# Two-layer hybrid encoder on one core: mixer A's projections and seven gate blocks in seven-product form, in a phase at the head of each layer

## The chip, the cores and the metric

One core of one Trainium2 chip runs the whole program. The metric is device microseconds of one execution, median of several runs.

## The reference

Two layers, 512 tokens, width 1024, all in float32. Each layer does this:

```
xn = rmsnorm(x, norm1_g[l]);  h = xn @ w_in[l]        # split into the inputs of four mixers
y_a = gdn_mixer(...)    # A: gated DeltaNet, q/k/v (512 columns each) through a 5-tap convolution and silu
y_b = diff_mixer(...)   # B: differential attention
y_c = swa_mixer(...)    # C: windowed attention
y_d = mlstm_mixer(...)  # D: mLSTM
branch = einsum('bsnw,nwd->bsnd', ys, w_branch[l])
gate   = sigmoid(einsum('bsd,dne->bsne', xn, w_gate[l]))
x = x + sum_n(gate * branch) @ w_out[l]
xn = rmsnorm(x, norm2_g[l]);  x = x + square(relu(xn @ w_mlp1[l])) @ w_mlp2[l]
```

A last rmsnorm follows. Every dense product `x @ w` of these is the subject here.

## The kernel before

**Dense products.** For precision each float32 operand is split into a high part and a low part; a product takes three matmuls (high x high, high x low, low x high). A weight block of 512 KB comes by DMA on SP's queue into a tile `wr` (two buffers), ScalarE copies it to the rounded high part `wh` (L292), VectorE subtracts to the low part `wl` (L293, "a split" below, in two pieces of 128x512 per block); `wh` and `wl` have three buffers each. `Item.get` (L244) gives a block and puts the splits of the next one (two ahead in the MLP) in the queues before it. The plain forms are `run_b` (L400; 128 columns, 24 matmuls of 512 tokens; q, k, v of mixer A), `run_b2` (L415; 256 columns, 48 matmuls of 512 tokens; gates `g`, branches `m`) and `run_a` (L374; 256 columns, 96 matmuls of 256 columns).

**The seven-product form.** The first MLP product (`M1`, L790) treats a group of 512 columns as 2x2 blocks of weights and 2x2 blocks of tokens and input halves, and makes it from seven products of half-size blocks in place of eight. Four weight blocks arrive in two large tiles `wq`; GpSimd makes the four combinations S1 to S4 (L809, two subtractions or additions of 128x512 each); the combinations T1 to T4 of the tokens are made once (`Norm.sums`, L492). Each product is 24 matmuls of 256 columns (L832 to L834); results are put together by six additions on VectorE (L850), one on GpSimd (L851) and two copies on ScalarE (L839).

**Order.** A list `ORDER` (L40) says in which order the dense items of a layer come. The letters: `ga0` is gate a, columns 0 to 255; `Ak0` mixer A's k projection, head 0; `sm` the small projections; `z`, `dv`, `do`, `dqk`, `B`, `C`, `Ck` the other mixers' projections; `gd` gate d; `ma`, `md` branch products with the gate (`m`); `xb`, `xc` gate and branch product in turn. Each item is a generator that gives 1300 or 1310 after each 1.3 us of matmuls. `until(label)` runs items up to a label. `drive(mixer)` runs a mixer: between its steps the mixer gives a gap in ns, and `fill` runs dense steps until the gap is paid. An item may wait for a mark (`dqk` for `s`, the end of mixer A's scans; `ma` for `ya`, the end of mixer A; likewise `md`, `mb`, `mc`); if the next item waits, `fill` gives nothing, and items behind it aren't looked at. The gaps, from `G` (L33) and the loops: mixer A 0.5, eight of 0.3, 2.5, four times 20 of 1.6, nine of 1.5, then 4 x 1.3 + 1.5 + 4 x 1.6 us; mixer D 57.1 in all; a half of mixer B 21.6, and some 9 to drain its transposes before the second; mixer C 73.9 (32 units, each a front and a step three units later of 0.95, and eight closings). The compiler then orders each engine's instructions from this program order, by what its own model says is ready; it may take a later instruction first where its data and buffers are there.

**The places of the change.** Before mixer A starts, `until("Aq3")` runs ga0, the q and k projections, `sm`, ga1 and ga2. `conv` (L942) copies a projection from PSUM, and runs the convolution: one scaled copy on ScalarE, four multiply-adds (L958) and, behind a tanh, a last step (L962) on VectorE. `merge` (L595) makes gates and branches; gate d's tanh goes to DRAM (L613) and comes back before `md`. Gates of b and c are used where they are made.

Of the kernel before, what the change touches and what calls it, by code (L numbers as in the profile page):

```python
# [10 lines left out]
F32 = mybir.dt.float32  # L11
# [6 lines left out]
P = 128  # L18
# [12 lines left out]
NAR = 26  # L31
NBG = 13
# [7 lines left out]
ORDER = ("ga0 Ak0 Aq0 sm ga1 Ak1 Ak2 Aq1 Aq2 Ak3 ga2 Aq3 Av z0 ga3 dv0 "  # L40
         "z1 dv1 do0 do1 gd dqk ma B0 Ck md B1 C0 C1 xb xc")
# [72 lines left out]
def encoder(ctx: ExitStack, tc: tile.TileContext, a: dict, out: bass.AP, dbg: dict = None):  # L114
# [8 lines left out]
    ar = ctx.enter_context(tc.tile_pool(name="ar", bufs=NAR))  # L123
    bg = ctx.enter_context(tc.tile_pool(name="bg", bufs=NBG))
# [112 lines left out]
    class Item:  # L237
# [285 lines left out]
    def build(l, L):  # L523
        w_in = a["w_in"][l]
        n1 = L.n1 = Norm(a["norm1_g"][l])
        L.n2 = Norm(a["norm2_g"][l], True)
        xf = lambda: n1.x

# [31 lines left out]
        def projA(kind, hs):  # L560
            for h in hs:
                def ev(ps, kind=kind, h=h):
                    conv(L, kind, h, ps)
                Item(f"A{kind}{h}{l}", wl_b(w_in, {"q": O_AQ, "k": O_AK, "v": O_AV}[kind] + h * P), run_b(xf, ev))
# [30 lines left out]
        def merge(n, key, part="gm", ccs=range(4)):  # L595
            yf = lambda: ([L.y[key][0][:, k, :] for k in range(4)], [L.y[key][1][:, k, :] for k in range(4)])
            for cc in ccs:
                st = {}

                def gev(b, bank, cc=cc, st=st):  # L600
                    kt = cc * 2 + b
                    if key == "a":
                        if kt == 0:
                            mgb = [B4(s="mg") for _ in range(2)]
                            L.mg = [mgb[k // 4][:, k % 4, :] for k in range(KD)]
                        act.activation(L.mg[kt], bank, AF.Tanh, scale=0.5)
                        return
                    sg = A(s="gs")
                    act.activation(sg, bank, AF.Tanh, scale=0.5)
                    if part == "g":  # L610
                        if key not in L.gsp:
                            L.gsp[key] = dr.tile([8, P, S], F32, tag=f"gs{key}{l}", name=f"gs{key}{l}")
                        act.dma_start(L.gsp[key][kt], sg)  # L613
# [3 lines left out]
                def bev(b, bank, cc=cc, st=st):  # L617
# [17 lines left out]
                f0 = key == "a" and cc == 0  # L635
                gi = lambda: Item(f"g{key}{cc}{l}", wl_a(a["w_gate"][l, :, n], cc * 256, KD),
                                  run_b2(xf, KD, gev, hook1 if f0 else None))
# [15 lines left out]
        bi = "abcd".index  # L653
        for o in ORDER.split():
            if o == "sm":
                small()
            elif o[0] == "A":
                projA(o[1], range(4) if len(o) == 2 else [int(o[2])])
# [131 lines left out]
        def M1(fg):  # L790
            st = {}
            qv = lambda t, i: t[:, i * 1024:(i + 1) * 1024].rearrange("p (k c) -> p k c", k=4)

            def slot(n):
                t, i = {"22": ("a", 0), "11": ("a", 1), "21": ("b", 0), "12": ("b", 1), "S3": ("b", 0),
                        "S1": ("a", 1), "S2": ("b", 0), "S4": ("b", 0)}[n]
                if t not in st:
                    st[t] = B(s="wq")
                return qv(st[t], i)

            def dma(n):
                i, j = int(n[0]) - 1, int(n[1]) - 1
                c0 = fg * 512 + i * 256
                nc.sync.dma_start(slot(n), w1[j * 512:(j + 1) * 512, c0:c0 + 256].rearrange("(k p) c -> p k c", p=P))

            def comb(dst, x, y, op):
                d, x, y = slot(dst), slot(x), slot(y)
                for k in range(0, 4, 2):
                    pool.tensor_tensor(d[:, k:k + 2], x[:, k:k + 2], y[:, k:k + 2], op=op)  # L809
            E = dict(kt=4, nc=256)  # L810
            pS3 = lambda: comb("S3", "11", "21", ALU.subtract)
            pS2 = lambda: comb("S2", "22", "S3", ALU.subtract)
            pS1 = lambda: comb("S1", "S2", "11", ALU.add)
            pS4 = lambda: comb("S4", "12", "S2", ALU.subtract)
# [936 lines left out]
```

## Time and profile before

| | |
|---|---|
| runs | 2354.01 us median of 3 (2350.83 to 2354.09) |
| the profiled execution's own time | 2351.57 us |
| its span (first to last instruction) | 2349.8 us |
| TensorE busy | 2285.3 us (97%) |
| VectorE, ScalarE, GpSimd busy | 1582.2, 1187.5, 747.6 us |
| granted TensorE clock | 0.996 of full speed |

In the rows below PE is TensorE, DVE VectorE, ACT ScalarE, POOL GpSimd, and L293 is line 293. Names stand as out<-in. A matmul's row gives 0.28 or 0.39 us, but matmuls are pipelined: the next one starts 0.12 or 0.23 us later.

### The profile page before, as it was taken

What the parts mean: (1) busy time and instruction counts of PE and PEld (TensorE: products, weight loads), DVE (VectorE), ACT (ScalarE), POOL (GpSimd) and SP (SyncE); (2) the same over time, 40 slices, a digit from 0 to 9 for tenths busy, and PEclk for the clock granted to TensorE, in tenths of its full rate; (3) what the DMA queues carried; (4) which work ended last, traced back from release to release, by engine and by line L of the source; (5) the groups of instructions that cost most, each with busy time, mean ns of one, the idle gap of its engine ahead of it and who ended that gap; (6) DMA issues with size and microseconds to landing.
All of it is one profiled execution on the core that took longest, in us unless ns stands there. A gap on an engine that the chain in (4) does not pass through costs nothing. (4 is left out here: it accounts for less than half of the span.)

```text
span 2349.8 us, 43335 instructions
## 1 busy us (share of the span) xinstructions
PE 2285.3 (97%) x16992; PEld 2083.2 (89%) x16992; DVE 1582.2 (67%) x2988; ACT 1187.5 (51%) x2777; POOL 747.6 (32%) x806
## 2 busy tenths in 40 slices
PE   7999999999999999999999999999999999999998
PEld 6879987989888989999987799879898889899998
DVE  5774547685786477677767745587767854867775
ACT  4565444654665264344445654365546643534443
POOL 1135552132232134343200555412313310434341
PEclk9999999999999999999999999999999999999999
DMA  6322131222122523333323112321221234233322
GB/s 149 99 46 64 55 95 57 60 88 80 51 71 74 160 71 122 95 109 108 111 74 90 55 55 64 91 63 52 93 82 55 72 106 131 90 97 109 99 82 90
DMA packets 234779, 200.72 MB, mean 85 GB/s; under 512 B 31696, under 2 KB 223824, under 8 KB 234576
## 3 DMA queue, kind: packets, MB, share of 16 engines
q1 hardware_dynamic: 231408, 192.75, 27.5%
q10 hardware_dynamic: 2304, 4.20, 0.5%
q8 instruction: 133, 2.18, 0.4%
q0 software_dynamic: 864, 1.02, 0.2%
q14 instruction: 70, 0.57, 0.1%
HBM read 190.04 MB, written 8.39 MB: 84 GB/s over the span
## 5 line engine op out<-in xcount | busy, mean ns | idle before, releaser
L293 DVE TENSOR_TENSOR wl<-wr,wh 128x512 fp32r<-128x512 f32 x540 | 400.4, 762 | 183.4 <-ACT wh L292 176.1
L292 ACT CAST wh<-wr 128x512 fp32r<-128x512 f32 x540 | 317.0, 621 | 219.0 <-PE pd L436 59.2
L392 PE MATMUL pd<-wh,xh 128*128 128x256 f32 x960 | 279.4, 291 | 0.0
L393 PE MATMUL pd<-wl,xh 128*128 128x256 f32 x960 | 269.8, 281 | 0.0
L394 PE MATMUL pd<-wh,xl 128*128 128x256 f32 x960 | 269.4, 281 | 0.0
L394 PE MATMUL pd<-wh,hl 128*128 128x256 f32 x896 | 248.2, 277 | 0.0
L392 PE MATMUL pd<-wh,hh 128*128 128x256 f32 x896 | 248.0, 277 | 0.0
L393 PE MATMUL pd<-wl,hh 128*128 128x256 f32 x896 | 248.0, 277 | 0.0
L292 ACT CAST wh<-wq 128x512 fp32r<-128x512 f32 x196 | 115.3, 619 | 220.4 <-PE pd L394 94.0
L435 PE MATMUL pd<-xh,wh 128*128 128x512 f32 (+1 forms) x544 | 217.7, 401 | 0.5 <-ACT xh L222 0.5
L436 PE MATMUL pd<-xl,wh 128*128 128x512 f32 (+1 forms) x544 | 209.0, 384 | 1.8 <-DVE xl L223 1.6
L437 PE MATMUL pd<-xh,wl 128*128 128x512 f32 (+1 forms) x544 | 208.8, 384 | 0.0
L293 DVE TENSOR_TENSOR wl<-wq,wh 128x512 fp32r<-128x512 f32 x196 | 181.9, 962 | 13.4 <-ACT wh L292 13.3
L393 PEld LDWEIGHTS pd<-wl,xh 128*128 128x128 f32 x960 | 181.9, 189 | 1.4
L392 PEld LDWEIGHTS pd<-wh,xh 128*128 128x128 f32 x960 | 181.5, 189 | 1.4
L394 PEld LDWEIGHTS pd<-wh,xl 128*128 128x128 f32 x960 | 181.3, 189 | 0.2
L809 POOL TENSOR_TENSOR wq<-wq,wq 128x512 f32<-128x512 f32 x84 | 124.4, 1488 | 163.1 <-DVE wl L293 153.7
L393 PEld LDWEIGHTS pd<-wl,hh 128*128 128x128 f32 x896 | 168.2, 188 | 0.0
L394 PEld LDWEIGHTS pd<-wh,hl 128*128 128x128 f32 x896 | 168.2, 188 | 0.0
L392 PEld LDWEIGHTS pd<-wh,hh 128*128 128x128 f32 x896 | 168.1, 188 | 0.0
L677 DVE TENSOR_TENSOR x<-pd,x 128x512 f32<-128x512 f32 x124 | 85.1, 689 | 101.4 <-PE pd L394 101.4
L1011 POOL TENSOR_TENSOR r<-r,r 128x512 f32<-128x512 f32 (+1 forms) x28 | 35.5, 1266 | 325.8 <-DVE r L1010 185.9
(394 smaller groups left out, 6656.9 us busy)
## 6 DMA issues: line engine op xcount, KB each, us to landing
wr<-in_w_in SPq DMA_DIRECT2D x92, 512.0 KB
wr<-in_w_mlp SPq DMA_DIRECT2D x72, 512.0 KB
wr<-in_w_gate SPq DMA_DIRECT2D x64, 512.0 KB
wq<-in_w_mlp SPq DMA_DIRECT2D x56, 512.0 KB
wr<-in_w_branch SPq DMA_DIRECT2D x32, 512.0 KB
wr<-in_w_out SPq DMA_DIRECT2D x16, 512.0 KB
x<-in_x SPq DMA_DIRECT2D x16, 256.0 KB
gsd<-gs ACTq DMA_DIRECT2D x16, 256.0 KB
```

The lines of the kernel that those rows point to most:

```text
L292: act.copy(wh[:, k:k + n], raw[:, k:k + n])
L293: dve.tensor_tensor(wl[:, k:k + n], raw[:, k:k + n], f(wh[:, k:k + n]), op=ALU.subtract)
L392: mm(o, th, wh[:, k4, :], start=(kt == 0 and tt % 2 == 0), stop=False)
L393: mm(o, th, wl[:, k4, :], start=False, stop=False)
L394: mm(o, tl, wh[:, k4, :], start=False, stop=(kt == kts - 1 and tt % 2 == 1))
L435: mm(o, w1_, xh[kt][:, sl], start=(kt == 0 and hi_ == 0), stop=False)
L436: mm(o, w1_, xl[kt][:, sl], start=False, stop=False)
L437: mm(o, w2_, xh[kt][:, sl], start=False, stop=last)
L677: dve.tensor_tensor(d, bank.rearrange("p (t c) -> p t c", t=2), d, op=ALU.add)
L809: pool.tensor_tensor(d[:, k:k + 2], x[:, k:k + 2], y[:, k:k + 2], op=op)
L1011: pool.tensor_tensor(v(t1), v(t1), v(t2), op=ALU.add)
```

## The change

M1's seven-product form becomes a function `SW` with a `begin`, a place for results and a `fin` per result block; the MLP uses it as before. Mixer A's q, k and v (`SAk`, `SAq`, `SAv`; 512 columns each) and seven-product gates use it too: `Sa1` (gate a, columns 512 to 1023; its columns 0 to 511 stay plain as `ga0`, `ga1`), `Sb0`, `Sb1` (gate b) and `Sc0` (gate c, first half; the second half stays plain as `xc2`, `xc3`). The first norm keeps its input in float32 (`Norm(..., True)`) and makes the sums T1 to T4 when ga1 starts. Results of q, k, v go straight into the convolution's padded input `ci`, now one large tile for four heads. Gates of b and of c's first half go to DRAM, as gate d does. Mixer A starts after `Sc0`. The lookahead of loads is 2 for these items. The pool of small tiles has 27 buffers in place of 26, the large one 14 in place of 13; the scratch for DMA descriptors is set to 4096 bytes; a tile of 480 bytes a partition, not used, is put between the two pools.

```diff
-NAR = 26
-NBG = 13
+NAR = 27
+NBG = 14
-ORDER = ("ga0 Ak0 Aq0 sm ga1 Ak1 Ak2 Aq1 Aq2 Ak3 ga2 Aq3 Av z0 ga3 dv0 "
-         "z1 dv1 do0 do1 gd dqk ma B0 Ck md B1 C0 C1 xb xc")
+ORDER = ("ga0 sm ga1 SAk SAq Sa1 Sb0 SAv Sb1 Sc0 z0 z1 dv0 dv1 do0 do1 gd Ck dqk ma B0 md B1 C0 C1 "
+         "mb mc0 mc1 xc2 xc3")
+    gap = ctx.enter_context(tc.tile_pool(name="gap", bufs=1))
+    gap.tile([P, 120], F32, name="gap")
-            la = G['la'] if self.label[:2] in ("m1", "m2") else 1
+            la = G['la'] if self.label[:2] in ("m1", "m2") or "src" in loads[i] else 1
-        n1 = L.n1 = Norm(a["norm1_g"][l])
+        n1 = L.n1 = Norm(a["norm1_g"][l], True)
+        def SW(label, w, col0, nrm, begin, dst, fin):
...
+                def last(i, j, bank, y, own):
+                    d = dst(i, j) if dst is not None else b2(y if own else A(s="c"))
+                    dve.tensor_tensor(d, b2(bank), b2(y), op=ALU.add)
+                    fin(d, i, j)
+                add = lambda d, x, y: dve.tensor_tensor(d, x, y, op=ALU.add)
+                p1 = cpy(prod(0, "11"))
+                yield 2600
+                p7 = cpy(prod(1, "T3"))
+                yield 2600
+                last(0, 0, prod(2, "21"), p1, False)
+                yield 2600
+                add(p1, prod(3, "T2"), p1)
+                pool.tensor_tensor(p7, p7, p1, op=ALU.add)
+                yield 2600
+                bank = prod(4, "T1")
+                last(1, 1, bank, p7, False)
+                add(p1, bank, p1)
+                yield 2600
+                last(1, 0, prod(5, "T4"), p7, True)
+                yield 2600
+                last(0, 1, prod(6, "22"), p1, True)
+                yield 2600
-        def projA(kind, hs):
...
+        def projA(kind):
...
+            def fin(d, i, j):
+                done.add((i, j))
+                if (i, 1 - j) in done:
+                    for h in (2 * i, 2 * i + 1):
+                        conv(L, kind, h, st[0][:, h])
+            SW(f"A{kind}3{l}", w_in, {"q": O_AQ, "k": O_AK, "v": O_AV}[kind], n1, begin, dst, fin)
+
+        def gateS(key, half):
...
+                act.activation(d, d, AF.Tanh, scale=0.5)
+                act.dma_start(gate_dram(key)[k:k + 2, :, cs].rearrange("k p c -> p k c"), d)
...
+                def run_g1(it, run_g=run_g):
+                    n1.sums()
+                    yield from run_g(it)
...
-                            for tp in range(2 if c < 4 else 0):
+                            for tp in range(2 if (key, c) in L.gsc else 0):
...
     def conv(L, kind, h, ps):
...
-        ci = A(s="ci", w=S + 4)
-        pool.memset(ci[:, 0:2], 0.0)
-        pool.memset(ci[:, S + 2:S + 4], 0.0)
-        act.copy(ci[:, 2:S + 2], ps)
...
-        until(f"Aq3{l}")
+        until(f"Sc0{l}")
...
-    nc = bacc.Bacc("TRN2", target_bir_lowering=False, num_devices=1)
+    nc = bacc.Bacc("TRN2", target_bir_lowering=False, num_devices=1, dynamic_dma_scratch_size=4096)
```

## Rows read from the trace of the kernel before

**Rows 1.** The page's first part: busy us (share of the span) xinstructions.
```profile
PE 2285.3 (97%) x16992; PEld 2083.2 (89%) x16992; DVE 1582.2 (67%) x2988; ACT 1187.5 (51%) x2777; POOL 747.6 (32%) x806
```
**Rows 2.** Table of stretches, layer 2: length, busy us by engine, clock, DMA share, GB/s.
```profile
1196.00:1266.00 70.00, 70.00 (x317) 57.51 (x316) 55.14 (x87) 38.89 (x66) 0.51 (x8) 1.00 0.32 91
...
1296.00:1332.00 36.00, 31.29 (x289) 26.93 (x288) 28.94 (x43) 22.81 (x58) 20.60 (x30) 1.00 0.20 59
...
1532.00:1552.00 20.00, 16.38 (x78) 13.12 (x79) 17.35 (x29) 8.53 (x15) 5.05 (x5) 1.00 0.17 53
...
1794.00:1897.00 103.00, 102.18 (x511) 83.98 (x511) 82.98 (x305) 70.63 (x241) 36.84 (x41) 1.00 0.22 67
```
**Rows 3.** Timeline of PE (start, us, what): first matmuls of two neighbouring plain blocks.
```profile
1225.88 0.39 PE L406 MATMUL pd<-xh,wh 128*128 128x512 f32 x1
...
1231.41 0.39 PE L406 MATMUL pd<-xh,wh 128*128 128x512 f32 x1
```
**Rows 4.** Timeline of PE: a seven-product item's first matmul, and the next item's.
```profile
951.98 0.28 PE L832 MATMUL pm<-xh,wh 128*128 128x256 f32 x1
...
971.81 0.28 PE L392 MATMUL pd<-wh,hh 128*128 128x256 f32 x1
```
**Rows 5.** Groups by line, whole span: count | busy us, mean ns | idle before, releaser.
```profile
L293 DVE TENSOR_TENSOR wl<-wq,wh 128x512 fp32r<-128x512 f32 x196 | 181.9, 962 | 13.4 <-ACT wh L292 13.3
...
L850 DVE TENSOR_TENSOR pp<-pm,pp 128x512 f32<-128x512 f32 x56 | 38.1, 679 | 0.0
```
**Rows 6.** Groups by line on DVE, stretch 1196 to 1266.
```profile
L958 DVE SCALAR_TENSOR_TENSOR ac<-ci,cw,ac 128x512 f32<-128x512 f32 x28 | 21.0, 751 | 2.9 <-ACT ac L956 2.0
L293 DVE TENSOR_TENSOR wl<-wr,wh 128x512 fp32r<-128x512 f32 x26 | 17.6, 687 | 8.9 <-ACT wh L292 8.8
L962 DVE SCALAR_TENSOR_TENSOR kb<-sg,ac 128x512 f32<-128x512 f32 x4 | 2.8, 690 | 0.9 <-DMA wr<-in_w_in 0.7
```
**Rows 7.** Timeline of PE: the MLP's first seven-product item, layer 1, and its successor.
```profile
864.10 0.28 PE L832 MATMUL pm<-xh,wh 128*128 128x256 f32 x1
...
888.53 0.28 PE L392 MATMUL pd<-wh,hh 128*128 128x256 f32 x1
```
**Rows 8.** Timeline of DVE and of POOL inside one seven-product item.
```profile
955.60 0.69 DVE L293 TENSOR_TENSOR wl<-wq,wh 128x512 fp32r<-128x512 f32 x1 [0.58 <-ACT wh L292]
...
958.38 2.43 DVE L293 TENSOR_TENSOR wl<-wq,wh 128x512 fp32r<-128x512 f32 x2 [0.16 <-ACT wh L292]
...
961.34 1.28 DVE L293 TENSOR_TENSOR wl<-wq,wh 128x512 fp32r<-128x512 f32 x2
...
958.37 1.29 POOL L809 TENSOR_TENSOR wq<-wq 128x512 f32<-128x512 f32 x1 [0.69 <-DVE wl L293]
```
**Rows 9.** Groups by line, whole span: the weight combinations on POOL.
```profile
L809 POOL TENSOR_TENSOR wq<-wq,wq 128x512 f32<-128x512 f32 x84 | 124.4, 1488 | 163.1 <-DVE wl L293 153.7
```
**Rows 10.** Timeline of PE in mixer A's scans, layer 2: scan matmuls, then dq's block.
```profile
1511.50 1.13 PE L1384 MATMUL pm<-vb,Y 128*128 128x128 f32 x8
1512.38 0.48 PE L406 MATMUL pd<-xh,wh 128*128 128x512 f32 x1
```
**Rows 11.** Groups by line on DVE, stretch 1794 to 1897 (mixer C, layer 2).
```profile
L223 DVE TENSOR_TENSOR ptl<-pm,pth 128x128 fp32r<-128x128 f32 x80 | 22.6, 284 | 3.7 <-ACT pth L222 3.4
...
L1602 DVE CUSTOM_DVE_ANT_0 cp<-pm,c_swnegr 128x256 f32<-128x256 f32 (+1 forms) x32 | 15.4, 482 | 0.6 <-PE pm L1598 0.2 <-POOL cp L1609 0.2
L1607 DVE TENSOR_TENSOR cst<-cst 128x1 f32<-128x1 f32 x32 | 8.4, 263 | 8.1 <-ACT cst L1606 7.9
L1638 DVE TENSOR_TENSOR ctmp<-pm,ctmp 64x256 f32<-64x256 f32 x16 | 6.7, 421 | 4.8 <-ACT ctmp L1637 4.7
L1604 DVE TENSOR_SCALAR cst<-cst,nsink 128x1 f32<-128x1 f32 x32 | 6.4, 203 | 0.1
...
L1608 DVE RECIPROCAL cst<-cst 128x1 f32<-128x1 f32 x32 | 4.9, 153 | 0.1
```
**Rows 12.** Timeline of ACT: a gate's tile is sent to DRAM.
```profile
1457.98 0.33 ACTq L613 DMA_DIRECT2D gsd<-gs  x1
```

More of the change, by code (lines that the diff above doesn't have):

```diff
@@ L558, in small, with begin, fin, gate_dram @@
             Item(f"small{l}", [dict(custom=small_load, kt=KD, nc=P)], run_b(xf, small_evac))
-        def projA(kind, hs):
[L561 to L564, printed above, removed]
+        def projA(kind):
+            st = {}
+            def begin():
+                setattr(L, kind + "b", B4(s=kind + "b"))
+                st[0] = B(s="ci", w=2080).rearrange("p (h c) -> p h c", h=4)
+                pool.memset(st[0][:, :, 0:2], 0.0)
+                pool.memset(st[0][:, :, S + 2:S + 4], 0.0)
+            dst = lambda i, j: st[0][:, 2 * i:2 * i + 2, 2 + j * 256:258 + j * 256]
+            done = set()
+            def fin(d, i, j):
[5 more added lines that the diff above has]
+        def gateS(key, half):
+            kt0 = 4 * half
+            def fin(d, i, j):
+                k = kt0 + 2 * i
+                cs = slice(j * 256, j * 256 + 256)
+                if key == "a":
+                    act.activation(L.mgb[half][:, 2 * i:2 * i + 2, cs], d, AF.Tanh, scale=0.5)
+                    return
+                act.activation(d, d, AF.Tanh, scale=0.5)
+                act.dma_start(gate_dram(key)[k:k + 2, :, cs].rearrange("k p c -> p k c"), d)
+                L.gsc.update(((key, 2 * half), (key, 2 * half + 1)))
+            SW(f"S{key}{half}{l}", a["w_gate"][l, :, bi(key)], half * 512, n1, lambda: None, None, fin)
+        def gate_dram(key):
+            if key not in L.gsp:
+                L.gsp[key] = dr.tile([8, P, S], F32, tag=f"gs{key}{l}", name=f"gs{key}{l}")
+            return L.gsp[key]
         def projD(kind, i):
@@ L603, in gev @@
                         if kt == 0:
-                            mgb = [B4(s="mg") for _ in range(2)]
+                            mgb = L.mgb = [B4(s="mg") for _ in range(2)]
                             L.mg = [mgb[k // 4][:, k % 4, :] for k in range(KD)]
@@ L610, in gev @@
                     if part == "g":
-                        if key not in L.gsp:
-                            L.gsp[key] = dr.tile([8, P, S], F32, tag=f"gs{key}{l}", name=f"gs{key}{l}")
-                        act.dma_start(L.gsp[key][kt], sg)
+                        L.gsc.add((key, cc))
+                        act.dma_start(gate_dram(key)[kt], sg)
                         return
@@ L656, in build @@
                 small()
-            elif o[0] == "A":
-                projA(o[1], range(4) if len(o) == 2 else [int(o[2])])
+            elif o[0] == "S":
+                projA(o[2]) if o[1] == "A" else gateS(o[1], int(o[2]))
             elif o[0] == "z":
@@ L806, in comb @@
[L806 to L814, printed above, removed]
@@ L874, in M1, with begin, sq @@
-            Item(f"m1_{fg}{l}", ents, run)
+            v = lambda t, i, j: t[:, 2 * i:2 * i + 2, j * 256:j * 256 + 256]
+            def begin():
+                L.h[fg] = (B4(F32R, "hh"), B4(F32R, "hl"))
+            def sq(r, i, j):
+                hh, hl = L.h[fg]
+                act.activation(r, r, AF.Relu)
+                act.activation(v(hh, i, j), r, AF.Square)
+                pool.tensor_tensor(r, r, r, op=ALU.mult)
+                dve.tensor_tensor(v(hl, i, j), r, f(v(hh, i, j)), op=ALU.subtract)
@@ L876, in M2 @@
+            SW(f"m1_{fg}{l}", w1, fg * 512, L.n2, begin, None, sq)
         def M2(fg):
```

128 lines of the change are left out of this document (51 added, 77 removed).

## The prediction

> **What bounds the kernel now.** I read the busy time of the engines first. TensorE is busy for 2285.3 of 2349.8 us [rows 1]; nothing else comes near. So the time is the sum of TensorE's instructions plus the little idle time between them, and a change can gain only by giving TensorE less to do, and lose only by letting it wait. The second view is a table of stretches of the second layer [rows 2]. Through the projections that open the layer (1196 to 1266) TensorE has no gap, but VectorE is busy for 55.1 of 70 us, the most of the other engines. Through mixer C (1794 to 1897) TensorE is full too, while VectorE is at 83 of 103 us. The kernel stays full because work of two kinds is interleaved: dense blocks, heavy for TensorE, and mixer steps, heavy for the other engines. At the end of mixer A (1532 to 1552) dense work is short, and TensorE loses 3.6 of 20 us.
>
> **What the change removes.** A block of 512 output columns costs four plain blocks of 24 matmuls. One of them goes from its first matmul at 1225.88 to the next block's at 1231.41 [rows 3], 5.53 us, so 22.1 us for 512 columns; the gate blocks have as many matmuls of the same width. The seven-product form has 168 matmuls of 256 columns, and the MLP already has items of exactly this form: one goes from 951.98 to 971.81 [rows 4], 19.8 us. That is 2.3 us saved for each of seven blocks a layer (three of mixer A, one of gate a, two of b, one of c), 14 in all: **-32 us**. The matmuls are pipelined, so I take distances from start to start, not durations.
>
> A smaller gain: before, the v projections and their convolutions run beside mixer A's first steps, and TensorE is idle for 4.7 of 36 us there (1296 to 1332) [rows 2]. They move to the front; 4 us a layer, **-8 us**.
>
> **What it adds in the front.** Between the first gate block and mixer A's start there are now ga0, the small block, ga1 and seven seven-product items. Per item VectorE has 14 splits (962 ns each in the MLP's items) and 6 additions from PSUM (679 ns) [rows 5]: 13.5 + 4.1 = 17.5 us, under the item's 19.8 us on TensorE. Mixer A's three items have the convolution on top: per head four steps of 751 ns and a last one of 690 ns [rows 6], for four heads 14.8 us, which makes 32.3 us on VectorE against 19.8 on TensorE. For the seven items: 7 x 17.5 + 3 x 14.8 = 167 us on VectorE against 7 x 19.8 = 139 on TensorE. A split may run only two loads ahead of its product (three pairs of split buffers), and the convolution stands in VectorE's queue ahead of the next item's splits, so the 28 us that are too many come out as waits of TensorE. Before, the same convolutions have plain blocks beside them with only 2 splits of 687 ns per 5.53 us [rows 6], and just fit.
>
> At its start the front also needs the four sums of token blocks, which the MLP needs too. There the first seven-product item behind the sums takes 864.10 to 888.53 [rows 7], 24.4 us, 4.6 more than a later one. I add 4.6. Front: 28 + 5 = 33 us a layer, **+66 us**.
>
> The unknown here is how often a split meets GpSimd. Two splits alone take 1.28 us; two that begin with a GpSimd subtraction take 2.43 us, 1.2 more, about the 1.29 us of that subtraction [rows 8]. The 962 ns are the mean over both cases. In the front GpSimd has eight subtractions of 1488 ns per item [rows 9] with no MLP second half between items to spread them. Low bound: every split at the 0.69 us of one that meets nothing [rows 8]: 7 x 13.7 + 44 = 140 us, 1 too many, with the start 6 us. High bound: GpSimd and VectorE always alternate on operands in SBUF: 11.9 + 9.7 = 21.6 us a gate item, 36.4 with the convolution, which is 7 x 21.6 + 3 x 14.8 - 139 = 57, with the start 61 us. I stay at 33, since the 962 ns are measured on the same item.
>
> By the Trainium skill, page GPSIMD Engine Reference, section 8 (Key points), GpSimd shares its SBUF interfaces with VectorE and contends with VectorE instructions that have two SBUF inputs; the pairs in [rows 8] agree, and the rule taken as strict exclusion is the high bound just given, 61 us a layer in place of 33. It speaks against this change, which puts more of both kinds side by side.
>
> **What it takes from the mixers.** The order is written so that a mixer asks for dense work in ns between its steps and gets it from the list; when the next item waits for a mark, nothing is given. I added up both sides from the listed gaps (a plain 256-column block counts 10.4). Per layer:
> - Mixer A wants 147 us up to its scans' mark and 13 after it. Before, Av, z, ga3, dv, do and gd give 136, and dqk behind the mark 21. After, z, dv, do, gd and Ck give 115, and dqk 21: 21 us less.
> - Mixer D wants 57 and finds 52: 5 short, before none.
> - Mixer B's second half wants 31, finds 21: 10 short, before none.
> - Mixer C wants 74. Before, mb, gb1 to gb3 and gc0 give 62 us. After, mb gives 21, and mc0 waits for mixer C itself: 53 short, before 12.
>
> Short is not lost, because the compiler's order takes matmuls from later items where their data are there: dq's blocks, listed behind the mark, run between the scans' steps [rows 10]. So the low bound is 0. The high bound is the whole further shortage, 77 us. For mixer C: one of three split buffers is free while mc0 and mc1 hold two, and lets gc2's halves through (10 us), as gc1 did before (hence no loss there); 43 stay short, that is 43/74 of 32 steps, 18.6. Such a step keeps VectorE for 64.4/32 = 2.0 us (six groups [rows 11]) and TensorE for 0.8 (the 103 us of the stage less 336 dense matmuls at 5.53/24 = 0.23 us leave 26 for 32 steps): 18.6 x 1.2 = 22 us. For mixer A I take half of 21, since dq covers the scans but then is missing from the tail, where TensorE loses 3.6 us even with it [rows 2]; half of the shortages of D and B likewise: 10, 3 and 5. Together 40 us a layer, **+80 us**.
>
> **What costs nothing.** The gates of b and of c's first half go to DRAM and back, 12 stores a layer on ScalarE's queue at 0.33 us of issue [rows 12]: 4 us, hidden by ScalarE's 31 free us of 70 in the front [rows 2]; without that cover, 4 us a layer. The 12 loads back stand in SP's queue ahead of mb's and mc's weights, each asked for one block (5.5 us) before its use; where one is late, mb waits, and that lies inside mixer C's bounds. The weights come as four loads of 512 KB per item as before, into the large pool. The fp32 copies of the normed input are eight ScalarE copies in the layer's tail, where the last MLP block covers them; at the program's start two pairs are bare, about 2 us, inside the bounds.
>
> **The sum.** -32 - 8 + 66 + 80 = +106 us on the profiled execution's 2351.6 us, or 2458; the median of the runs, 2354.0, is 2.4 above it, so 2460. Bounds: 2354 - 40 + 2 x 6 = 2326 and 2354 - 40 + 2 x (61 + 77) = 2590.
>
> **The rivals.** About 0.2% (4.7 us) is what a measurement of this kernel can tell from no change.
> 1. Only the front costs: the compiler's order fills the mixers. For it: dq in [rows 10]. Against: mc0 and ma hold the weight buffers ahead of anything free. 2354 - 40 + 66 + 10 = 2390. Chance 0.18.
> 2. Strict alternation of GpSimd and VectorE: 2354 - 40 + 2 x (61 + 40) = 2516. Chance 0.10. Against: a mean of 962 ns [rows 5] lies nearer to 690 than to the 690 + 1200 of a split that collides, so most don't. By the rule of the Trainium skill's page GPSIMD Engine Reference, section 8, it would be this rival.
> 3. Faster: splits seldom meet GpSimd and the convolutions yield to them. It decides where VectorE's work of the seven items falls under TensorE's 139 us, that is at splits under 0.69 us; the mixers then lose 2 us a layer. 2354 - 40 + 2 x (6 + 2) = 2330. For it: the MLP's items lose nothing once they run. Against: they have a plain half between them, and no convolution. Chance 0.15.
> 4. No difference: waits of some 20 us a layer eat the 40. The change then does less work and waits for it. Chance 0.05.
>
> My forecast has 0.52; its own range is 2410 to 2510. The range 2345 to 2550 takes in rivals 1, 2 and 4 and leaves out rival 3 and the far end, 0.2 together. Faster is rival 3, 0.15; within 0.2% rival 4, 0.05; slower the rest, 0.80.
>
> **What would show it.** TensorE's sum should fall by some 32 us while the span grows. In the stretch of the seven items the waits of the seven-product matmuls should be for VectorE's splits, worst behind Ak, Aq and Av, and an A item should last some 30 us, a gate item near 20. In mixer C TensorE should be idle for 20 us a layer, with VectorE ending the waits. Gate items well over 20 us speak for rival 2; a full TensorE in mixer C for rival 1. I am wrong if the A items run in 20 us.

## The result and the profile after

The changed kernel takes **2594.53 us** (median of 4 runs, 2593.29 to 2595.23) against 2353.82 before (4 runs, 2350.83 to 2354.09): ratio 1.103, 95% interval [1.101, 1.104]. It is slower, as forecast, but by 241 us where the prediction said 106 (2460, with a range up to 2550). The profiled execution took 2594.12 us, its span is 2592.4, so 242.6 more than before. First the page's line of busy times, which answers to [rows 1]:

```profile
PE 2339.6 (90%) x18000; PEld 2167.5 (84%) x18000; DVE 1789.8 (69%) x3180; ACT 1258.0 (49%) x2897; POOL 930.7 (36%) x896
```

TensorE's sum should have fallen by 32 us and rose by 54. Next the table of stretches of the second layer in the order front, mixer A, D, B, C, the dense work behind C, MLP (start and end, length, then the busy time and instructions of PE, its weight loads, DVE, ACT and POOL, the granted clock, and the DMA share and GB/s), of the kernel after and then of the kernel before. The "front" is all that runs ahead of mixer A.

```profile
1308.00:1557.00 249.00, 186.93 (x1383) 180.23 (x1382) 213.40 (x260) 113.88 (x204) 103.91 (x75) 0.86 0.25 76
1557.00:1825.00 268.00, 257.25 (x2312) 224.99 (x2311) 143.06 (x251) 135.24 (x341) 129.50 (x172) 0.99 0.20 61
1825.00:1918.00 93.00, 87.51 (x634) 81.40 (x634) 69.03 (x164) 57.00 (x165) 14.75 (x12) 0.98 0.24 75
1918.00:2066.00 148.00, 133.92 (x949) 122.92 (x948) 96.10 (x206) 72.72 (x171) 33.04 (x32) 0.95 0.22 68
2066.00:2144.00 78.00, 64.80 (x280) 47.75 (x278) 66.37 (x280) 53.72 (x208) 35.61 (x40) 0.87 0.17 55
2144.00:2247.00 103.00, 99.33 (x670) 90.37 (x671) 58.78 (x87) 40.04 (x80) 17.45 (x14) 0.98 0.41 128
2247.00:2585.00 338.00, 335.17 (x2771) 332.92 (x2770) 236.52 (x323) 145.44 (x262) 127.78 (x96) 0.99 0.29 93
```

```profile
1184.00:1271.00 87.00, 86.76 (x436) 72.84 (x435) 62.47 (x104) 44.40 (x79) 2.73 (x18) 1.00 0.33 92
1271.00:1555.00 284.00, 274.18 (x2346) 237.75 (x2345) 167.02 (x271) 144.10 (x358) 135.37 (x178) 1.00 0.21 64
1555.00:1656.00 101.00, 96.90 (x723) 90.71 (x722) 72.80 (x171) 61.16 (x173) 15.55 (x13) 1.00 0.23 68
1656.00:1794.00 138.00, 135.51 (x988) 124.72 (x988) 99.17 (x212) 76.17 (x178) 35.05 (x32) 1.00 0.25 75
...
1897.00:2010.00 113.00, 111.94 (x727) 100.43 (x726) 60.10 (x92) 44.22 (x87) 17.46 (x15) 1.00 0.40 126
2010.00:2343.00 333.00, 330.04 (x2765) 327.62 (x2764) 236.50 (x323) 144.54 (x261) 126.29 (x96) 0.99 0.30 94
```

(Mixer C of before stands in [rows 2]: 103 us, TensorE full.) The work itself must be taken off before these are compared. Into the front come seven items of 19.8 us, out of it go eight plain blocks and ga2 (8 x 5.53 + 11): 83 us more. It grew by 162, so **79 us are lost** there. Av and ga3 (33 us) left mixers A and D, which shrank by 24: **9 lost**. Gate b and half of gate c (66 us) left the rest; B and the MLP grew by 15, C and the work behind it shrank by 35: **46 lost**. Less the 16 saved this is the layer's 118; the first layer has the other 125. Not all that is lost is idle time. In mixers A and D TensorE's idle time (length less busy time) grew by 2 us only, and in the stretches from B on by 26; the other 7 and 20 us are busy time above what the work asks for, much of it where the granted clock is lower (0.95 in B, 0.87 in C).

What TensorE waits for, over the span (view of the waits: engine, line, releaser, us in total, times, longest):

```profile
PE pm L574 <- ACT pp L581: 87.5, 6, 15.5
PE pm L1187 <- DVE sq L1181: 24.2, 10, 3.7
PE pm L574 <- ACT xsh L224: 23.2, 2, 11.6
...
PE pm L576 <- DVE wl L295: 13.6, 17, 2.8
```

L574 to L576 are the seven-product matmuls, L581 the ScalarE copy `pp` of a product out of PSUM, L224 the cast of a token sum, L295 the split; L1187 belongs to the end of mixer B, of which more below. I had expected the splits; they end 13.6 us of waits, and the copies 87.5. The seven items one by one, k, q, gate a, b0, v, b1, c0 (table of stretches, each from an item's first matmul to the next item's):

```profile
1338.91:1376.64 37.73, 23.47 (x169) 22.67 (x168) 32.49 (x48) 18.54 (x33) 10.51 (x9) 0.77 0.27 85
1376.64:1416.27 39.63, 23.29 (x171) 22.47 (x169) 33.67 (x41) 13.61 (x24) 14.71 (x12) 0.78 0.14 40
1416.27:1453.84 37.57, 23.33 (x170) 22.51 (x169) 30.82 (x40) 14.68 (x26) 13.81 (x12) 0.82 0.22 70
1453.84:1473.63 19.79, 19.79 (x171) 19.79 (x169) 19.59 (x18) 10.76 (x19) 15.90 (x11) 1.00 0.26 82
1473.63:1493.56 19.93, 19.93 (x170) 19.87 (x169) 19.80 (x22) 10.23 (x18) 12.49 (x8) 1.00 0.25 75
1493.56:1535.39 41.83, 24.84 (x171) 24.22 (x169) 34.84 (x42) 15.40 (x27) 15.86 (x10) 0.76 0.12 41
1535.39:1555.34 19.95, 19.95 (x172) 19.95 (x171) 18.60 (x20) 12.95 (x24) 10.07 (x7) 1.00 0.24 76
```

An item with no convolution behind it from its predecessor takes 19.8, as forecast. The three behind k, q and v (that is q, gate a and b1; "the long items" below) have the predecessor's convolution beside them; they take 38 to 42 and lose 60 us, and the first item loses 18. v's own item, behind a gate, takes 19.9. Each long item holds one wait of 13.5 to 15.5 us, and these waits are on ScalarE's queue (timeline of ACT; in brackets the idle time before and what ended it):

```profile
1383.42 0.63 ACT L991 ACTIVATE sg<-ac 128x512 f32<-128x512 f32 x1 [3.20 <-DVE ac L989]
1383.96 0.71 ACT L987 ACTIVATE ac<-ci,cw 128x512 f32<-128x512 f32 x1
1384.58 2.69 ACT L294 CAST wh<-wq 128x512 fp32r<-128x512 f32 x5
1393.90 0.63 ACT L991 ACTIVATE sg<-ac 128x512 f32<-128x512 f32 x1 [6.64 <-DVE ac L989]
...
1404.11 0.63 ACT L991 ACTIVATE sg<-ac 128x512 f32<-128x512 f32 x1 [3.18 <-DVE ac L989]
1404.65 1.05 ACT L581 COPY pp<-pm 128x512 f32<-128x512 f32 x2
```

ScalarE stands idle before each of the four tanhs `sg` of k's convolution (one is left out above), and the copies of q's first two products, which TensorE finished at 1379 and 1382, come right behind the last tanh. TensorE meanwhile fills its four PSUM banks and stops from 1389 to 1405.

### The profile page after: what moved, and what is told of

Read it like the earlier page. It is cut to its first block, busy times and chain, and to the rows that moved or that the text cites. A ratio compares the mean times of both kernels' runs of the same rounds, so it can differ in the third digit from the quotient of the medians.

```text
span 2592.4 us, 46025 instructions
## 1 busy us (share of the span) xinstructions
PE 2339.6 (90%) x18000; PEld 2167.5 (84%) x18000; DVE 1789.8 (69%) x3180; ACT 1258.0 (49%) x2897; POOL 930.7 (36%) x896
## 4 chain that ended last, share of the span: by engine, by line
PE 71%; DVE 16%; ACT 4%; issue 4%; POOL 3%; DMA 1%; SPq 0%; POOLq 0%; DVEq 0%; ACTq 0%
PE pd L394 8%; PE pd L395 8%; PE pd L396 8%; PE pm L574 5%; PE pm L575 5%; PE pm L576 5%; DVE wl L295 4%; PE pd L437 4%; PE pd L438 4%; PE pd L439 4%; DVE ac L989 3%; PE pm L1592 1%; POOL r L1042 1%; PE pd L409 1%; PE pd L408 1%
## 5 line engine op out<-in xcount | busy, mean ns | idle before, releaser
L295 DVE TENSOR_TENSOR wl<-wr,wh 128x512 fp32r<-128x512 f32 x428 | 315.8, 763 | 132.3 <-ACT wh L294 131.5
L295 DVE TENSOR_TENSOR wl<-wq,wh 128x512 fp32r<-128x512 f32 x392 | 376.1, 993 | 21.0 <-ACT wh L294 20.6
L574 PE MATMUL pm<-xsh,wh 128*128 128x256 f32 x896 | 262.4, 293 | 110.6 <-ACT pp L581 87.5
L551 POOL TENSOR_TENSOR wq<-wq,wq 128x512 f32<-128x512 f32 x168 | 259.3, 1556 | 266.9 <-DVE wl L295 230.6
L574 PEld LDWEIGHTS pm<-xsh,wh 128*128 128x128 f32 x896 | 179.1, 200 | 112.3 <-ACT pp L581 88.7
L575 PE MATMUL pm<-xsl,wh 128*128 128x256 f32 x896 | 261.4, 292 | 5.3 <-DVE xsl L225 5.2
L576 PE MATMUL pm<-xsh,wl 128*128 128x256 f32 x896 | 261.2, 292 | 1.9 <-DVE wl L295 1.9
L576 PE MATMUL pm<-xh,wl 128*128 128x256 f32 x672 | 192.7, 287 | 11.8 <-DVE wl L295 11.7
L574 PE MATMUL pm<-xh,wh 128*128 128x256 f32 x672 | 191.1, 284 | 0.0
L575 PE MATMUL pm<-xl,wh 128*128 128x256 f32 x672 | 191.0, 284 | 0.0
L575 PEld LDWEIGHTS pm<-xsl,wh 128*128 128x128 f32 x896 | 178.8, 200 | 6.5 <-DVE xsl L225 6.5
```

The source lines that it names most:

```text
L295: dve.tensor_tensor(wl[:, k:k + n], raw[:, k:k + n], f(wh[:, k:k + n]), op=ALU.subtract)
L574: mm(o, w1_, xh[k], start=(k == 0 and b == 0), stop=False)
L575: mm(o, w1_, xl[k], start=False, stop=False)
L576: mm(o, w2_, xh[k], start=False, stop=(k == 3 and b == 1))
```

## The experiments

Each time below is that of one execution, beside one of the kernel before on the same chip (2352 to 2357 us). An item's time is the distance from its first matmul to the next item's, in the second layer.

One part of the time goes its own way. In the MLP each seven-product item is followed by 192 plain matmuls. They take some 22 or some 23 us, with TensorE busy throughout and the granted clock at 1.00; here in the changed kernel and in e14 (below), each time behind the second item:

```profile
2327.31:2350.14 22.83, 22.83 (x194) 22.83 (x193) 14.23 (x22) 6.88 (x12) 6.87 (x6) 1.00 0.26 88
```

```profile
2317.52:2339.27 21.75, 21.75 (x194) 21.75 (x193) 14.35 (x22) 6.88 (x12) 6.44 (x6) 1.00 0.29 93
```

The matmuls start 0.118 or 0.113 us apart; what decides which, no run shows. The five later items with their plain parts take 208 and 210 us in the two layers before, 212 and 212 after, and 207 to 214 a layer in the runs below. So up to 13 us between two times can come from this alone, and I go by the stretches where I can.

**Whose tile?** My theory 1 was that a copy `pp` is given the small tile that the convolution before it gives back last. Two edits let the copies go ahead of the tanhs: e1 takes the convolution out of the small pool, e5 gives `pp` a pool of its own out of the same bytes (the unused tile goes too).

```diff
-        ac = A(s="ac")
+        ac = getattr(L, kind + "b")[:, h, :]
...
-        sg = A(s="sg")
+        sg = ci[:, 0:S]
```

> Edit: the convolution works in place (sum in the result's own slice, tanh in the padded input that is dead by then), so that it takes no tile of the small pool; same instructions, same sizes. Theory 1 (buffers): the two ScalarE copies pp of a seven-product item take small tiles that the convolution before them gives back, so they stand behind its last tanh in ScalarE's queue, TensorE fills its four PSUM banks and waits some 15 us, three times a layer. Then here the six waits for pp (87.5 us) fall under 15 us, the second layer's front goes from 248 to about 215 us (VectorE has 213 us of work there, which becomes the bound), and the time falls by 60 to 80 us, to 2515 to 2535. Rival 1 (VectorE alone, as the prediction had it): the waits only change their name, from pp to wl; front over 240, time over 2575.

```diff
-NAR = 27
+NAR = 24
...
+    pq = ctx.enter_context(tc.tile_pool(name="pq", bufs=3))
...
-                    t = A(s="pp")
+                    t = pq.tile([P, S], F32, tag="pq", name=nm("pp")) if label[0] != "m" else A(s="pp")
```

> Edit: the copies pp of the front's seven-product items get a pool of three tiles of their own; the small pool gives three up (24 left), so that no byte is added. The convolution keeps its tiles. Theory 1 (a copy pp waits since it gets the very tile that the convolution before it gives back last): the copies now stand ahead of the convolution's tanhs in ScalarE's queue; the waits for pp (87.5 us) all but vanish, items behind an A item go from 38 to 42 us to the 33 to 35 that VectorE's work in them takes, time 2555 to 2570 as with the convolution in its own room. Rival (there are too few small tiles): the rest has three tiles fewer, so the waits grow, time 2600 or more.

e1: 2565.1. e5: 2582.6. Both are above what I expected. Both lose the waits for `pp`, and in both the three long items take 104 us together, in place of 119. Of e1 these are (table of stretches), and its longest waits of TensorE:

```profile
1367.40:1402.12 34.72, 23.11 (x171) 22.32 (x170) 32.87 (x41) 13.73 (x24) 15.59 (x10) 0.80 0.15 46
1402.12:1435.45 33.33, 23.74 (x171) 22.95 (x169) 30.79 (x39) 14.28 (x25) 16.64 (x13) 0.80 0.26 79
...
1476.04:1512.07 36.03, 22.53 (x171) 21.73 (x169) 34.50 (x42) 15.40 (x27) 16.84 (x10) 0.81 0.14 49
```

```profile
PE pm L574 <- ACT wh L294: 46.9, 6, 9.8
```

Now VectorE (third busy time) is full in them: 98 of 104 us (100 of 104 in e5). Theory 1 holds, at half its size: 29 us, 28 of them in the front. The waits that are left in e1 still end on ScalarE's queue, where a cast `wh` now stands behind a tanh; but that tanh waits for VectorE's convolution steps, and VectorE has no room left. So what bounds these items now is VectorE's own work. The cause isn't the number of tiles, since e5 has three fewer for everything else. Its seven items take within 2 us of what e1's take; the rest of it is longer, and of the 17 us that it takes more than e1 half lie in the MLP's later items and plain parts. Where the others come from I didn't test. A consistent gap that repeats can mean that SBUF or PSUM has no room for the next tile, says the Trainium skill (Perfetto Trace Analysis, Optimization Strategy); here the room was there, and the copy waited for the tile that it was given.

**VectorE's work.** e2 leaves out the convolution, e3 GpSimd's weight combinations in the front; e11 is e3 with the edits of e1 and e5 as well.

```diff
-        ac = A(s="ac")
...
-        dve.scalar_tensor_tensor(dst, sg, 1.0, ac, op0=ALU.add, op1=ALU.mult)
+        act.activation(dst, ci[:, 2:S + 2], AF.Copy, scale=cw[:, 2, ft:ft + 1])
```

> Left out: the convolution of q, k and v; one scaled ScalarE copy per head stands in its place (VectorE loses 60 instructions a layer). Theory 1: without convolution no copy pp is held up; the seven items run at the rate of the gate items, 20 to 22 us each, front of the second layer 180 to 190 us, time 2460 to 2485; what is left above the kernel before (some 110 us) is then the gate items, the start of the front and the mixers. Rival 2 (every seven-product item of the front is slow by GpSimd against VectorE, convolution or not): items of 24 us and more, front over 200, time over 2500.

```diff
             def comb(dst, x, y, op):
+                if label[0] != "m":
+                    return
                 d, x, y = slot(dst), slot(x), slot(y)
```

> Left out: GpSimd's eight weight combinations per seven-product item in the front (56 a layer); the MLP keeps its own. Rival 2 (contention of GpSimd and VectorE is what makes the front long): splits fall from 1033 to 690 ns and convolution steps from 1003 to 750, VectorE's 213 us in the second layer's front to about 167, and the front goes to 175 to 190 us, time 2450 to 2480. Theory 1: VectorE's work falls likewise, but the copies pp still stand behind the convolution, now shorter: waits of 9 to 12 us each, front 205 to 225 us, time 2510 to 2550.

> Edit: the change with both mends of the tiles (the convolution in its own room, the copies pp in a pool of their own), and GpSimd's weight combinations of the front left out. Theory: with no wait for a tile left, an item lasts as long as VectorE's instructions in it; without collisions those are 14 splits at 0.69, 4 or 6 additions and 4 convolutions at 3.7 us, 25 to 28 us. Items behind an A item: 25 to 29 us (31 with the combinations left out alone), the others 19.8; time 2510 to 2525. Rival (ScalarE's queue order still holds them): items of 31, 2535 or more.

e2: 2475.6, every item behind the first 19.8 to 20.9; the seven items of the second layer fall from 216 to 159 us. q's item, of 39.63 us in the change, in e2:

```profile
1318.67:1338.45 19.78, 19.78 (x170) 19.78 (x169) 19.58 (x20) 10.95 (x20) 13.48 (x9) 1.00 0.26 79
```

VectorE spends about as much on the convolutions there (48.1 + 8.2 us), but that the two agree is in part chance: its busy time in the seven items falls by 38 us only (190 to 151), and the other 19 are the waits behind the tanhs, 15 of which e1 showed to be the tile's. e3: 2541.9, the long items 31, as theory 1 had it. q's item and the gate item b0 in e3:

```profile
1346.19:1377.12 30.93, 21.46 (x170) 21.25 (x169) 25.94 (x41) 13.73 (x24) 1.28 (x1) 0.83 0.17 51
...
1407.96:1427.74 19.78, 19.78 (x170) 19.78 (x169) 13.83 (x20) 11.09 (x20) 1.60 (x1) 1.00 0.28 84
```

The gate item now leaves VectorE 6 us free, yet none of the long items' work moves there: they still hold 25 to 26 us of it. e11: 2533.7, 9 us above expectation, the long items 27.8 to 29.1, at the upper end of it; gate a's item, behind q's convolution, in e11:

```profile
1371.85:1400.95 29.10, 23.41 (x171) 22.71 (x169) 25.66 (x39) 14.05 (x25) 1.69 (x3) 0.82 0.30 91
```

What the collisions add is seen in the groups by line on DVE in the second layer's front, of the change and of e3 (rows: splits, convolution steps):

```profile
L295 DVE TENSOR_TENSOR wl<-wq,wh 128x512 fp32r<-128x512 f32 x98 | 98.1, 1033 | 2.7 <-ACT wh L294 2.5
L989 DVE SCALAR_TENSOR_TENSOR ac<-ci,cw,ac 128x512 f32<-128x512 f32 x48 | 48.1, 1003 | 0.5
```

```profile
L295 DVE TENSOR_TENSOR wl<-wq,wh 128x512 fp32r<-128x512 f32 x98 | 69.0, 730 | 12.9 <-ACT wh L294 12.9
L991 DVE SCALAR_TENSOR_TENSOR ac<-ci,cw,ac 128x512 f32<-128x512 f32 x48 | 35.9, 748 | 0.5
```

29 + 12 us of VectorE's time a layer are collisions, and the front gets 30 us shorter without them: 26 in the three long items, 4 in the first. Nothing is paid elsewhere: the gate items take 19.8 with and without the combinations. A single collision, in the timelines of DVE and of POOL:

```profile
1387.43 0.74 DVE L989 SCALAR_TENSOR_TENSOR ac<-ci,cw,ac 128x512 f32<-128x512 f32 x1
...
1389.80 1.75 DVE L989 SCALAR_TENSOR_TENSOR ac<-ci,cw,ac 128x512 f32<-128x512 f32 x1
...
1389.28 3.38 POOL L551 TENSOR_TENSOR wq<-wq,wq 128x512 f32<-128x512 f32 x2
```

The Trainium skill (SBUF — State Buffer, "SBUF: two separate sides") calls the port pair that VectorE and GpSimd share an exclusive lock: whichever starts first holds it for its whole instruction, and the other blocks. The rows agree as to the single instruction (1.75 us in place of 0.74 for the step that starts inside a subtraction of 1.7).

**The start.** Gate a's quarter ga2 (e6), then ga3 as well (e9), stand plain ahead of the first seven-product item; gates b and c are plain as in e4 below, and mixer A starts behind `SAv`.

The lists of e4, e6 and e9:

```diff
-ORDER = "ga0 sm ga1 SAk SAq Sa1 SAv z0 z1 dv0 dv1 do0 do1 gd dqk ma B0 Ck md B1 C0 C1 xb xc"
+ORDER = "ga0 sm ga2 ga1 SAk SAq SAv z0 ga3 z1 dv0 dv1 do0 do1 gd dqk ma B0 Ck md B1 C0 C1 xb xc"
+ORDER = "ga0 sm ga2 ga1 ga3 SAk SAq SAv z0 z1 dv0 dv1 do0 do1 gd dqk ma B0 Ck md B1 C0 C1 xb xc"
```

> Edit, on the kernel with gates b and c plain: gate a's columns 512 to 767 come plain between the small projections and ga1 (which makes the sums of token blocks), its last 256 plain in mixer A as before; q, k, v stay seven-product items one behind the other. Theory: the first item takes 38 us in place of 19.8 because the sums' sixteen tiles wait for the tiles of the small projections' chain; with 11 us of plain work between them that wait goes: first item 20 to 22, 17 us a layer. The items for q and v stay at 37 to 42, behind the convolutions of k and q. Mixer A gets 11 us of cover back. From 2487: - 34 + 5 (plain in place of seven products) - 5 = 2445 to 2460. Rival (the first item is slow whatever stands before it, by its loads or the chain on VectorE): 2480 or more.

> Edit, on e6: ga3 stands between ga1 and k's item as well, so that 11 us more of plain work pass between the sums and the first seven-product item; mixer A loses them. Theory: what is left of the first item's excess (29.5 in place of 19.8) is VectorE's work for the sums, some 13 us, and is covered now: first item 20 to 22, 8 to 9 us a layer. Mixer A gives back about 5 a layer for 11 us less cover. 2466 - 18 + 10: 2450 to 2465. Rival (the first item is slow by its own loads): first item 27 and more, 2470 or more.

e6: 2466.5, first item 29.5; I had expected 20 to 22 there. e9: 2458.4, first item 19.7, as expected. In the changed kernel VectorE has made the sums by 1325.6, but their casts `xsh` stand in ScalarE's queue behind the chain of the small projections (timeline of ACT):

```profile
1340.06 0.62 ACT L950 COPY LG<-val 8x512 f32<-8x512 f32 x1 [3.12 <-DVE val L947]
...
1349.92 0.61 ACT L979 COPY CO<-m 8x512 f32<-8x512 f32 x1 [2.10 <-DVE m L964]
...
1351.81 4.26 ACT L224 CAST xsh<-xf 128x512 fp32r<-128x512 f32 x8
```

So the first item loses 18 us to sums whose casts come late, and the 22 us of ga2 and ga3 ahead of it cover this; e6 gave half of that and got half. Whether the order in the queue is a matter of tiles here too was not tried.

**Fewer items, with room.** e7: a plain 256-column item behind each of k, q and v. e8: v plain. e12: q plain too. All have e1's convolution.

Their lists in this order (mixer A starts behind `SAv`, `SAq` and `Aq`):

```diff
+ORDER = "ga0 sm ga2 ga1 SAk ga3 SAq z0 SAv z1 dv0 dv1 do0 do1 gd dqk ma B0 Ck md B1 C0 C1 xb xc"
+ORDER = "ga0 sm ga2 ga1 SAk ga3 SAq Av z0 z1 dv0 dv1 do0 do1 gd dqk ma B0 Ck md B1 C0 C1 xb xc"
+ORDER = "ga0 sm ga2 ga1 SAk Aq Av z0 ga3 dv0 z1 dv1 do0 do1 gd dqk ma B0 Ck md B1 C0 C1 xb xc"
```

> Edit, on the one before: the convolution in its own room, and one plain 256-column item behind each seven-product item (ga3 behind k, z0 behind q, z1 behind v). Theory (a seven-product item has all of VectorE's time for itself, 19.6 of 19.8 us, so a convolution beside it comes on top; a plain item has VectorE free for 8 of 11 us): pairs of an A item and a plain item take 31 to 35 us in place of 37 to 42 + 11, some 15 us less for each of two pairs a layer; time 2375 to 2400. Rival (the seven-product form in the front is slow for another reason than VectorE): pairs of 45 and more, 2430 or more.

> Edit: only k and q are seven-product items, with a plain item behind each; v plain in mixer A as before; every gate plain; the convolution in its own room. Theory: with VectorE's time given room, and the sums behind plain work, each item keeps its 2.3 us: 4 items, -9 us against the kernel before, less what the cover of mixer A loses (ga3 stands in the front: 11 us, of which I take 3 to 5 a layer): 2345 to 2365. Rival (the form costs more than it saves wherever a convolution stands behind it): 2375 or more.

> Edit: k alone is a seven-product item, q plain behind it, v plain in mixer A, all gates plain, the order of before otherwise; the convolution in its own room. VectorE's budget of the front: before, 55 of 70 us; the item adds 12 us of splits and additions and the sums 13, against 15 free in 70 and 5 more in the rest of the stretch. Theory: short by 5 to 10 us a layer, against 2.3 saved: 2360 to 2375. Rival (room enough): 2346 to 2352, the 4.6 us saved.

Measured 2439.2, 2407.6 and 2380.2: all above what I expected (e7's first two pairs took 40.3 and 35.9 us). One item a layer still costs 26 us in all, two 55, three 87 (the MLP's later items and plain parts make 3 to 5 of each). The pair of k's item and ga3 in e8 (first stretch) and k's item in e12 (second) show why:

```profile
1257.31:1298.23 40.92, 35.39 (x217) 32.38 (x216) 39.33 (x52) 19.12 (x35) 11.30 (x9) 0.87 0.10 26
```

```profile
1239.27:1266.59 27.32, 22.61 (x170) 22.20 (x169) 26.29 (x32) 13.38 (x24) 11.43 (x11) 0.88 0.07 18
```

VectorE is full (39.3 of 40.9, 26.3 of 27.3). An item takes 2.3 us from TensorE and gives VectorE 14 splits where four plain blocks have 8, six additions, and its share of the sums; in a front where VectorE was busy for 62 of 87 us the 25 left are just what one item and the sums ask for by my count (12 + 13), and not all of them lie beside that item. This is an argument: no run measures the sums' share by itself. No version that I ran beats the kernel before.

**The mixers.** e4 has gates b and c plain at their old places. e10 moves only gate b's first half to the front. e13 keeps the change and puts gate c's plain half, which waits for no mark, ahead of `mb`.

The change's list, then e10's and e13's (e4's stands above):

```diff
-ORDER = ("ga0 sm ga1 SAk SAq Sa1 Sb0 SAv Sb1 Sc0 z0 z1 dv0 dv1 do0 do1 gd Ck dqk ma B0 md B1 C0 C1 "
-         "mb mc0 mc1 xc2 xc3")
+ORDER = "ga0 sm ga1 SAk SAq Sa1 Sb0 SAv z0 z1 dv0 dv1 do0 do1 gd dqk ma B0 Ck md B1 C0 C1 mb0 mb1 xb2 xb3 xc"
+ORDER = "ga0 sm ga1 SAk SAq Sa1 Sb0 SAv Sb1 Sc0 z0 z1 dv0 dv1 do0 do1 gd Ck dqk ma B0 md B1 C0 C1 gc2 gc3 mb mc"
```

> Edit: gates b and c in the plain form at their old places (each beside its branch product, after mixer B's and C's projections); mixer A's q, k, v and gate a's second half stay seven-product items of the front. Front cost and mixer cost apart: the mixers B and C get their cover back. By the stages of the changed kernel (TensorE idle in B, C and after C 28 us a layer more than before) the mixers cost 25 to 30 us a layer and the front the rest; three gate items less in the front, which ran at 20 to 24 us against 22.1 plain, change nothing else. Then 2594 - 2 x 28 + 6 x 2.3 less any clock given back: 2535 to 2555. If the mixers' idle time costs nothing (rival 1 of the prediction): 2590 or more. If the gate items in the front are themselves slow: under 2520.

> Edit, on the kernel with gates b and c plain (2487): gate b's columns 0 to 511 alone are a seven-product item of the front (behind gate a's, so behind no convolution), the rest of b and all of c plain beside their branch products. Theory (cover): mixer C's gaps want 74 us and now find some 50, against 62 with all gates there and 21 in the change; TensorE's idle time there goes to 3 to 7 us a layer, between 1 and 14, and the granted clock falls there for part of it; the gate item itself runs in 20 us. Time 2495 to 2510. Rival (mixer C's loss is not from cover, but from the loads of the gates or from the order of B0, Ck): no idle time in C beyond 2 us, 2480 to 2488.

> Edit, on the change: gate c's second half, plain, stands as two items of its own ahead of mb (its tanh goes to DRAM and comes back like the first half's), in place of beside its branch product behind mc1; nothing else. These 22 us wait for no mark. Theory (the loss at the end of mixer B is that every listed item left there waits for a mark): TensorE's idle time in B falls from 14 to 2 to 4 us a layer, that in C from 14 to 8 to 12, and the granted clock comes back with them: 20 to 25 us a layer, time 2540 to 2560. Rival (the loss is in the loads of the gates, which are now more): 2590 or more.

e4: 2487.2, 48 below the lower end of what I expected; I had overlooked that with b1 gone nothing of the seven-product form stands behind v's convolution, so the 41.8 us item goes as well (22 us a layer). TensorE's idle time in B and C is back at 2.3 and 1.1 us. e10: 2528.1, above expectation, and the loss is elsewhere than I put it: TensorE is idle for 2.6 us in C, but for 14.8 in B, as in the whole change (14.1). e13: 2536.5, a little better than expected. Its stretches of B and C:

```profile
1887.00:2021.00 134.00, 132.31 (x959) 122.17 (x959) 93.70 (x205) 72.50 (x169) 33.13 (x31) 1.00 0.24 73
2021.00:2107.00 86.00, 76.01 (x368) 59.40 (x366) 72.42 (x291) 59.89 (x222) 35.65 (x41) 0.95 0.32 108
```

So at the end of mixer B, where its output is normalised and transposed, gate b was the only work next in the list that waits for no mark. In the changed kernel TensorE waits there four times (view of the waits in the stretch 1918 to 2066), in e13 not at all:

```profile
PE pm L1187 <- DVE sq L1181: 11.5, 4, 3.7
```

Moving 22 us of work a layer to another place in the list is worth 58 us. 47 of them lie between the front and the MLP: 28 are TensorE's idle time, most of it in B, and 19 its busy time, with the granted clock at 1.00 in B in place of 0.95 and at 0.95 in C in place of 0.87. e14 puts two matmuls that nobody reads into each gap that finds no work (`keep[0]` is a tile of the normed input while mixer B's second half and C run); e15 joins e13 and e1.

```diff
             if r is None:
                 debt[0] = 0.0
+                if keep[0] is not None:
+                    t = PSD()
+                    for i in range(2):
+                        mm(t, identr, keep[0], start=(i == 0), stop=(i == 1))
                 return
```

> Edit, on the change: where mixer B's second half or mixer C asks for dense work and the next item waits, two matmuls of 512 columns into a bank that nobody reads are put there (0.46 us at full clock); the rest is the same. Theory (some 28 us a layer in the mixers are not idle time but matmuls at half the clock, after idle time): TensorE is busy through the gaps, its granted clock in mixer C goes from 0.87 to 0.95 and more, and the stretch from mixer B to the MLP gets 5 to 15 us a layer shorter although more is computed: 2565 to 2585. Rival (the clock is not set by idle time, or the added matmuls hold the mixer up): no gain or a loss, 2592 to 2620.

> The bridge of the run above and the convolution in its own room (2594 to 2565 when it was alone), both on the change. Theory (front and mixers are apart): the two gains add up to within 10 us; the front is as in e1 (234 us in the second layer), the mixers as in the run above: 2510 to 2530. If they share a cause: 2540 or more.

e14: 2578.3. Mixer C of e14:

```profile
2056.00:2134.00 78.00, 75.15 (x368) 58.63 (x367) 66.38 (x279) 53.16 (x207) 35.00 (x40) 0.98 0.17 55
```

The clock is back (0.98 in place of 0.87) and C takes the 78 us of the changed kernel, so here it gained nothing in C. That TensorE doesn't set the pace there is not shown by this: the added matmuls fill it to 75 of 78 us, and GpSimd's waits for TensorE in C grow from 3 to 10 us. B gets 4 us shorter and the work behind C 3 longer. The rest of the 16 us is in the MLP, 8 in the second layer; 5 of these 8 are its plain parts at 22 in place of 23 us, which isn't the granted clock (1.00 in both). e15: 2511.1; 29 + 58 = 87 were to be had and 83 came, so front and mixers are separate causes. Its seven items take what e1's take, and its way from the front to the MLP what e13's takes (680 us in the second layer).

## Why the prediction was wrong

- **-32 for the products:** right for an item that nothing disturbs: 19.8 us, gate items in the front too. So rival 2 (strict alternation everywhere, 21.6 us a gate item) is out. But collisions cost more than the prediction gave them where a convolution is: the convolution steps took 1003 ns in place of 751, for it let only the splits collide.
- **-8 for Av and the shortage of mixers A and D** (a net +9 a layer): 9 in the second layer. The number came, the mechanism only in part: these were to be idle time of TensorE, which grew by 2 us. So the number is luck in part.
- **The front, 33 a layer, measured 79.** The step that failed is "7 x 17.5 + 3 x 14.8 = 167 us on VectorE against 7 x 19.8 = 139 on TensorE", in two ways. It let the gate items' slack pay for the convolutions. But splits run two loads ahead and no more, and a gate item already has VectorE busy for 19.6 of 19.8 us. Even where e3 gives it 6 us of slack, nothing carries over: each convolution is paid in the item that runs beside it. VectorE's 32.3 us for an item with a convolution was near (30.8 to 34.8 in the long items); these three, less 3 x 19.8, make 40 us, not 28. And an item was taken to last as long as its busiest engine. It lasted 6 to 7 us longer, 20 a layer, since the copies `pp` stood behind the tanhs: the sign that I named was waits for the splits, and the waits were for ScalarE. e1 and e5 show that 15 of the 20 are the tile's.
- **The start, 4.6, measured 18:** taken from the MLP, where no chain of small projections stands in ScalarE's queue ahead of the sums' casts. That this chain is the reason is read from the timeline; e6 and e9 show that plain work ahead of the item covers it.
- **The mixers B and C, 27 a layer, measured 46.** TensorE's idle time grew by 26 us from B to the MLP, near the 27, but in other places: C's idle time was 13 us where I said 20; B's end, put at 5, was 12 (e13). The other 20 are busy time: 3 of them are the MLP's plain parts, much of the rest the clock.
- **A term was missing: the clock.** TensorE's busy sum is 86 us above what the work asks for (54 + 32), where the prediction wanted it to fall. It isn't all price: with the clock kept up in C the stage is no shorter (e14). In the long items it shows as 23.3 us busy for 19.8 us of matmuls.
- **"I am wrong if the A items run in 20 us"** came true of one of the three: v's item took 19.9, k's 37.7 and q's 39.6. And "a gate item near 20" failed for gate a (37.6) and b1 (41.8). What makes an item long is the convolution of the item before it, not its own kind.
- **The range.** Its upper end left out the far end of my own bounds, 2590, and the time lies above even that. The front's 79 us lie above the 61 of its upper bound, which held no term for the tile (15) and had the start at 4.6 (18).

## What to carry to other kernels

A form that saves TensorE a tenth is only worth taking where the other engines have room for what it adds: add up VectorE's time item by item, and let slack of one item pay for another only as far as the loads run ahead. When a wait repeats, look at what stands ahead of the releasing instruction in its own engine's queue, and whose tile it writes to; give what TensorE waits for tiles that slow work doesn't hold. Before moving work out of a stage, see which of it was the only work there that waits for nothing. And look at the parts that no edit touches: here the MLP alone moved by up to 13 us from run to run.

## What the runs showed of the hardware

- After the three long waits of the second layer's front TensorE's clock is at the lower of its two levels (1.2 of 2.4 GHz): the matmuls from 1405.27 on are 0.21 us apart, those before the wait 0.12. The front has 0.86 over all, mixer C 0.87. With added matmuls that nobody reads it stayed at 0.98 in C (e14). That activity gives the clock back is what the Trainium skill says (TensorE: Matmul & The Clock Gate, Part 1), and these rows agree; what I had not expected is that C got no shorter by it.
- A VectorE instruction with two operands in SBUF waits out most of the GpSimd instruction that it meets, the convolution step (0.74 to 1.75 us) as much as the split (0.68 to 1.78 at 1388.09).
- The same 192 matmuls of 128x256 take 21.75 or 22.83 us at a granted clock of 1.00 and with no wait of TensorE. Which of the two a part gets is open.
